# Where the stationary weight parts of the half-size matmuls begin in their buffers: four offsets become one

## Chip, cores and metric

The kernel runs on one core of a Trainium2 chip. The metric is the device time of one execution in microseconds (us), the median of several runs; lower is better. Three runs of the kernel before took 853.28, 854.75 and 855.66 us, so the median is 854.75 us.

## What is computed

One layer of a streaming encoder: a SwiGLU feed-forward block, a mixer (chunked attention beside a pooling branch), a second feed-forward block and a last norm, on 512 tokens of width 1024, with an inner width of 2816, all in float32.

```python
def swiglu_ffn(x, w_gate, w_up, w_down):
    return (jax.nn.silu(x @ w_gate) * (x @ w_up)) @ w_down

x = x + 0.5 * swiglu_ffn(rmsnorm(x, ffn1_norm[l]), ffn1_w_gate[l], ffn1_w_up[l], ffn1_w_down[l])
x = x + hybrid_mixer(rmsnorm(x, mix_norm[l]), w_in[l], q_norm[l], k_norm[l], rel_bias[l],
                     pool_w[l], pool_scale[l], w_out[l])
x = x + 0.5 * swiglu_ffn(rmsnorm(x, ffn2_norm[l]), ffn2_w_gate[l], ffn2_w_up[l], ffn2_w_down[l])
x = rmsnorm(x, final_norm[l])
```

The change touches the products `x @ w_gate` and `x @ w_up` of both feed-forward blocks.

## The kernel before

**High and low parts.** A float32 operand is split into a high part (rounded to the matmul's type, by ScalarE: `nc.scalar.copy`) and a low part (the remainder, by VectorE). A product of two operands is then three matmuls, `mm3` (lines 190 to 192): high by high, high by low, low by high. The first operand of each is stationary (loaded into TensorE by a weight load, "PEld" in the profile), the second moves through.

**The half-size up products.** The inner width has 22 panels of 128 columns. The first five (`PLAIN`) are multiplied as they stand: the weights are stationary, 128x128, and 512 tokens move. The other 17 of each block use a Strassen scheme (the Winograd form): seven products of half size in place of eight, where 128x128 weight parts are stationary and only 256 columns move. One pass of the loop over n (17 passes in each of the two feed-forward blocks) is called a block of matmuls here: seven products of 4 steps `k` of 3 matmuls, 84 matmuls. The weight operands of a block are four tiles, made by `high` (ScalarE, line 487) and `low` (VectorE, line 492):

- part 11: 512 columns, for the product A11
- part 13: 1024 columns (a sum of two quadrants), for S3 and S1
- part 24: 1024 columns (sums again), for S2 and A22
- part 22: 1024 columns, for A12 and S4

TensorE runs the products in the order A11 (part 11), S3 (13), S2 (24), A22 (24), S1 (13), A12 (22), S4 (22). Their moving operands are A11, A22, S1 and A12 in tiles that the profile calls `ha` (pool `norm`), S3 and S2 in `xa` (pool `resid`), and S4 in `sa` (the activations' pool). Outputs alternate between banks `mm` and `a`, so a profile row tells the products apart: `mm<-ha` is A11, S1 or A12, `a<-xa` S3, `mm<-xa` S2, `a<-ha` A22, `mm<-sa` S4.

**Buffers and order.** The four parts of a block take turns over four pairs of buffers of 1152 elements (`part_tiles`): three pairs in the pool `weights`, the fourth in the activations' pool (`act1` or `act2`), which begins behind the pool `small`. With four parts and four buffers, each part has the same buffer and the same offset in all 17 blocks of a layer. The order of all engines in this loop is written out by hand. While TensorE works on block n, ScalarE and VectorE prepare the parts of block n+1, and SyncE fetches the raw weights of block n+2 (two DMAs of 512 KB, lines 479 and 480, into two `raw` buffers in turn). GpSimd starts DMAs that add up weight panels in DRAM for the down products (line 720).

**The down products** come after the loop: there the tokens (`ah`) are stationary and the weight parts move, 512 columns at a time; these parts start at offset 0 of the same buffers.

Of the kernel before, what the change touches and what calls it, by code (L numbers as in the profile page):

```python
# [8 lines left out]
F32 = mybir.dt.float32  # L9
# [7 lines left out]
P = 128  # L17
# [18 lines left out]
HILO = 3  # L36


ROOM, STEPS = 1024 + 128, (16, 32, 64, 8)
PLAIN = 5  # L40
PROBS = 3
M_TILES = 16
# [25 lines left out]
def layer(  # L68
# [37 lines left out]
    tpool = ctx.enter_context(tc.tile_pool(name="temp", bufs=8))  # L106
    small = ctx.enter_context(tc.tile_pool(name="small", bufs=2))
    ps = ctx.enter_context(tc.tile_pool(name="ps", bufs=4, space=PSUM))
    dram = ctx.enter_context(tc.tile_pool(name="scratch", bufs=1, space=bass.MemoryType.DRAM))

    n_tiles = [0]
# [3 lines left out]
    def name(what):  # L115
        n_tiles[0] += 1
        return f"{what}_{n_tiles[0]}"

    def temp(dtype=F32):
        return tpool.tile([P, S], dtype, tag="t", name=name("t"))  # L120
# [43 lines left out]
    part_rooms: list = [(wpool, HILO)]  # L164
    n_parts = [0]

    def part_tiles(steps=(0,)):

        pool, bufs = part_rooms[n_parts[0] % len(part_rooms)]
        at = steps[n_parts[0] % len(steps)]  # L170
        n_parts[0] += 1
        return (
            pool.tile([P, ROOM], F32R, tag=tag, name=name("w" + tag), bufs=bufs)[:, at : at + 1024]
            for tag in ("hi", "lo")
        )

    def weights(src, parts=1):
        n = src.shape[-1]
        raw = raw_tile()
        hi, lo = part_tiles()  # L180
        for i in range(parts):
            part = slice(i * n // parts, (i + 1) * n // parts)
            nc.sync.dma_start(raw[:, part], src[:, part])
            split(raw[:, part], hi[:, part], lo[:, part])
        return hi, lo
# [240 lines left out]
    def ffn_up(norm, wA, down, loaded):  # L426
# [56 lines left out]
                )  # L483

        def high(n, what, src):
            hi, lo = (z[:, : src.shape[-1]] for z in part_tiles(STEPS))
            nc.scalar.copy(hi, src)  # L487
            w[what] = hi, lo, src

# [8 lines left out]
        def high11(n):  # L498
            if n < KF:
                high(n, (n, 11), raws[n][:, :S])  # L500
# [18 lines left out]
        def high13(n):  # L519
            if n < KF:  # L520
                high(n, (n, 13), w[n, "odd"])
# [5 lines left out]
        def high24(n):  # L527
            if n < KF:
                high(n, (n, 24), w[n, "even"])
# [61 lines left out]
        with tc.manual_schedule(engines={E.PE, E.DVE, E.Activation, E.SP}):  # L591
            last_silu = last_place = last_sums = nothing
            for n in range(PLAIN, KF):
                f = down.order[n]
                acc, up_lo, up_hi = bank()[:, :HT], bank()[:, :HT], abank()[:, :HT]
                u, z, sg = temp(), temp(), temp()
# [66 lines left out]
    class Down:  # L663
# [85 lines left out]
        def weights(self, i, g):  # L749

            if (i, g) in self.parts:
                return self.parts.pop((i, g))
            if (i, g) not in self.raws:
                self.fetch(i, g)
            src, raw = self.rows(i, g), self.raws.pop((i, g))
            n = groups[g][1] * S
            hi, lo = part_tiles()
            if tuple(src.shape[1:]) == (groups[g][1], S):
                split(raw, hi[:, :n], lo[:, :n])
            else:  # L760
                split(
                    raw.rearrange("p (d k c) -> p k d c", d=S // P, c=P),
                    *(z[:, :n].rearrange("p (k d c) -> p k d c", d=S // P, c=P) for z in (hi, lo)),
                )
            return hi, lo
# [722 lines left out]
    with tc.tile_pool(name="act2", bufs=1, reuse_waits="tile") as apool:  # L1488
        down2.begin(apool)

        for half in range(2):
            for t in range(NT):
# [5 lines left out]
                z = temp()  # L1498
# [229 lines left out]
```

## Time and profile before

| what | value |
|---|---|
| median of 3 runs | 854.75 us |
| the profiled execution's own time | 854.88 us |
| its span, first to last instruction | 852.9 us |
| granted TensorE clock | 0.998 of full speed |
| TensorE busy (matmuls) | 842.5 us, 99% |
| VectorE busy | 713.0 us, 84% |
| ScalarE busy | 502.0 us, 59% |
| GpSimd busy | 117.5 us, 14% |
| half-size blocks, first layer | from about 61.5 to 233 us of the span |
| half-size blocks, second layer | from about 569.5 to 739 us |

Read it from TensorE: its share of busy time is 99%, and in the chain of work that ended last 93% is TensorE. A matmul's busy time overlaps that of the next one, so what counts is not how long one is busy, but the distance from the start of one matmul to the start of the next. The timeline gives the starts in steps of 0.01 us.

### The profile page before, as it was taken

To read this page: it belongs to the slowest core of one execution; us is meant where nothing else is said; L and a number is where in the kernel's file an instruction comes from. 1 tells how busy PE (TensorE), PEld (TensorE's weight loads), DVE (VectorE), ACT (ScalarE), POOL (GpSimd) and SP (SyncE) were. 2 spreads that over 40 slices of the span, in tenths; PEclk is the share of its full clock that TensorE was granted. 3 is DMA by queue.
4 is the path that set the end of the run, shared out by engine and by line. 5 is a ranking of instruction groups with operands and counts; after the bars stand their busy time and mean duration, and the time that the engine had idled before them with its cause. 6 is when DMAs were issued, how large, how long until landed. Compare 5 with 4: busy or idle time off the path is not lost.

```text
span 852.9 us, 14106 instructions
## 1 busy us (share of the span) xinstructions
PE 842.5 (99%) x5288; PEld 757.1 (89%) x5288; DVE 713.0 (84%) x1122; ACT 502.0 (59%) x859; POOL 117.5 (14%) x196
## 2 busy tenths in 40 slices
PE   9999999999999999999999999999999999999996
PEld 8889999999988888887888888889999999978886
DVE  7998889888897868776979668988888888787896
ACT  7445555555576657458747746355555555666573
POOL 0124322222000000101111000122211111122000
PEclk9999999999999999999999999999999999999999
DMA  8199998877576864332212117249778767899832
GB/s 295 55 269 266 293 271 201 195 196 200 136 243 199 269 202 135 112 111 87 75 69 71 60 50 271 102 111 257 219 195 242 173 191 218 254 317 350 265 110 99
DMA packets 72244, 158.50 MB, mean 186 GB/s; under 512 B 6112, under 2 KB 29168, under 8 KB 71792
## 3 DMA queue, kind: packets, MB, share of 16 engines
q1 hardware_dynamic: 49088, 110.93, 37.5%
q0 software_dynamic: 22656, 46.14, 24.9%
q8 instruction: 41, 0.67, 0.3%
q10 hardware_dynamic: 432, 0.54, 0.2%
q14 instruction: 27, 0.22, 0.1%
HBM read 153.38 MB, written 50.34 MB: 239 GB/s over the span
## 4 chain that ended last, share of the span: by engine, by line
PE 93%; DMA 2%; DVE 2%; ACT 1%; issue 1%; SPq 0%; ACTq 0%; DVEq 0%
PE mm L190 22%; PE mm L191 22%; PE mm L192 22%; PE a L191 7%; PE a L192 7%; PE a L190 7%; DMA raw<-in_wA_dram 2%; PE a L1288 1%; PE a L1224 1%; PE a L1276 1%; DVE wlo L492 1%; PE a L227 0%; PE a L1495 0%; DVE wlo L146 0%; PE a L1146 0%
## 5 line engine op out<-in xcount | busy, mean ns | idle before, releaser
L145 ACT CAST whi<-raw 128x1024 fp32r<-128x1024 f32 (+2 forms) x115 | 107.4, 946 | 57.5 <-PE mm L191 17.0
L146 DVE TENSOR_TENSOR wlo<-raw,whi 128x1024 fp32r<-128x1024 f32 (+2 forms) x115 | 124.2, 1089 | 20.3 <-ACT whi L145 19.9
L191 PE MATMUL mm<-ha,whi 128*128 128x256 f32 x408 | 115.5, 283 | 0.0
L192 PE MATMUL mm<-ha,wlo 128*128 128x256 f32 x408 | 115.0, 282 | 0.0
L190 PE MATMUL mm<-ha,whi 128*128 128x256 f32 x408 | 114.9, 282 | 0.0
L583 ACT ACTIVATE t<-mm 128x256 f32<-128x256 f32 x102 | 39.2, 384 | 120.9 <-PE mm L192 120.1
L492 DVE TENSOR_TENSOR wlo<-wsum,whi 128x1024 fp32r<-128x1024 f32 x68 | 83.0, 1220 | 13.8 <-ACT whi L487 13.7
L192 PEld LDWEIGHTS mm<-ha,wlo 128*128 128x128 f32 x408 | 77.3, 189 | 0.0
L190 PEld LDWEIGHTS mm<-ha,whi 128*128 128x128 f32 x408 | 77.2, 189 | 0.1
L191 PEld LDWEIGHTS mm<-ha,whi 128*128 128x128 f32 x408 | 77.1, 189 | 0.1
L190 PE MATMUL mm<-hhi,whi 128*128 128x512 f32 x192 | 75.6, 396 | 0.0
L191 PE MATMUL mm<-hlo,whi 128*128 128x512 f32 x192 | 75.0, 391 | 0.0
L192 PE MATMUL mm<-hhi,wlo 128*128 128x512 f32 x192 | 74.7, 391 | 0.0
L720 POOL DMA_DIRECT2D wsum<-in_wB_dram x72 | 70.4, 1148 | 11.7 <-issue 8.2
L487 ACT CAST whi<-wsum 128x1024 fp32r<-128x1024 f32 x68 | 68.0, 1048 | 2.9 <-PE mm L191 2.7
L191 PE MATMUL mm<-wlo,ah 128*128 128x512 f32 x176 | 68.6, 390 | 0.0
L192 PE MATMUL mm<-whi,ah 128*128 128x512 f32 x176 | 68.5, 389 | 0.0
L190 PE MATMUL mm<-whi,ah 128*128 128x512 f32 x176 | 68.4, 390 | 0.0
L492 DVE TENSOR_TENSOR wlo<-raw,whi 128x512 fp32r<-128x512 f32 x68 | 62.6, 951 | 4.7 <-ACT whi L487 4.7
L718 POOL COPY mark<-t 128x1 f32<-128x1 f32 x40 | 14.1, 353 | 378.9 <-DVE t L628 229.6
L487 ACT CAST whi<-raw 128x512 fp32r<-128x512 f32 x68 | 56.3, 828 | 11.4 <-DMA raw<-in_wA_dram 11.4
L146 DVE TENSOR_TENSOR ah<-acts,ah 128x512 fp32r<-128x512 f32 (+1 forms) x72 | 45.7, 641 | 16.3 <-ACT ah L145 15.9
(228 smaller groups left out, 2378.5 us busy)
## 6 DMA issues: line engine op xcount, KB each, us to landing
raw<-in_wA_dram SPq DMA_DIRECT2D x87, 512.0 KB, 5.6
wsum<-in_wB_dram POOLq DMA_DIRECT2D x60, 512.0 KB, 7.5
raw<-wsum SPq DMA_DIRECT2D x40, 512.0 KB, 4.5
raw<-in_wB_dram SPq DMA_DIRECT2D x30, 512.0 KB, 4.7
wsum<-wsum POOLq DMA_DIRECT2D x20, 512.0 KB, 5.6
x<-in_xT_dram SPq DMA_DIRECT2D x16, 256.0 KB, 6.0
raw<-in_wQK_dram SPq DMA_DIRECT2D x8, 512.0 KB, 3.5
raw<-in_wO_dram SPq DMA_DIRECT2D x8, 512.0 KB, 3.4
```

Of the source, the lines that this page charges most:

```text
L145: nc.scalar.copy(hi, src)
L146: nc.vector.tensor_tensor(lo, src, hi.bitcast(F32), op=ALU.subtract)
L190: nc.tensor.matmul(acc, a[0], b[0], start=start, stop=False, **more)
L191: nc.tensor.matmul(acc, a[0], b[1], start=False, stop=False, **more)
L192: nc.tensor.matmul(acc, a[1], b[0], start=False, stop=stop, **more)
L487: nc.scalar.copy(hi, src)
L492: nc.vector.tensor_tensor(lo, src, hi.bitcast(F32), op=ALU.subtract)
L583: nc.scalar.activation(dst, src, AF.Copy, scale=scale)
L718: nc.gpsimd.tensor_copy(mark, after[:, 0:1])
L720: nc.gpsimd.dma_start(self.rows(i, g), self.rows(self.terms[i][at], g), **(dict(accum_op=ALU.add) if at else {}),)
L1224: nc.tensor.matmul(banks[i][:, at : at + n], qT[pair][0][a][rows, t * P : (t + 1) * P], kT[pair][0][b][rows, :n], start=a + b == 0, stop=a ...
L1276: nc.tensor.transpose(tp[:, n : n + P], prob[h, t][:, j * P : (j + 1) * P], ident)
```

## The change

The four offsets by turns become one: each part of the half-size products begins 16 elements (64 bytes) into its buffer. A tile of 64 float32 (256 bytes per partition) that nothing uses is set aside in the pool `small`, so that all that lies behind it, the activations' pool among it, moves up by 256 bytes.

```diff
-ROOM, STEPS = 1024 + 128, (16, 32, 64, 8)
+ROOM, AHEAD_OF_PARTS, ALIGN = 1024 + 128, 16, 64
...
     ps = ctx.enter_context(tc.tile_pool(name="ps", bufs=4, space=PSUM))
+    small.tile([P, ALIGN], F32, tag="align", name="align", bufs=1)
...
-    def part_tiles(steps=(0,)):
+    def part_tiles(at=0):
         pool, bufs = part_rooms[n_parts[0] % len(part_rooms)]
-        at = steps[n_parts[0] % len(steps)]
         n_parts[0] += 1
...
         def high(n, what, src):
-            hi, lo = (z[:, : src.shape[-1]] for z in part_tiles(STEPS))
+            hi, lo = (z[:, : src.shape[-1]] for z in part_tiles(AHEAD_OF_PARTS))
```

No instruction is added, removed or moved: on every engine the same instructions stand in the same order, and only addresses differ. In bytes per partition, as the two programs place them:

| operand | buffer | offset before, after | start modulo 512 before, after |
|---|---|---|---|
| part 11 (A11) | `weights` | 256, 64 | 128, 448 |
| part 13 (S3, S1) | activations' pool | 32, 64 | 160, 448 |
| part 24 (S2, A22) | `weights` | 64, 64 | 448, 448 |
| part 22 (A12, S4) | `weights` | 128, 64 | 0, 448 |
| moving `sa` (S4) | activations' pool | 0, 0 | 128, 384 |
| moving `ha`, `xa` | `norm`, `resid` | 0, 0 | 384, 384 |
| all else in the activations' pool and the mixer's, which takes its place | | | 128, 384 |

High and low tiles of a part start alike modulo 512. Part 24 is the one whose start stays where it was.

## Prediction

> **What bounds the kernel now.** I began with the page's table of busy time, then took busy time by stage, to see where TensorE ever waits. The first row below is the page's; the other three are stages, with their length, then the busy time of PE, PEld, DVE, ACT and POOL, the clock, the DMA share and GB/s.
>
> ```profile
> PE 842.5 (99%) x5288; PEld 757.1 (89%) x5288; DVE 713.0 (84%) x1122; ACT 502.0 (59%) x859; POOL 117.5 (14%) x196
> ...
> 70.50:82.30 11.80, 10.17 (x85) 9.97 (x85) 9.00 (x14) 5.40 (x11) 4.02 (x6) 1.00 1.10 309
> ...
> 112.50:232.00 119.50, 119.50 (x1009) 119.50 (x1008) 103.72 (x145) 66.82 (x121) 24.66 (x36) 1.00 0.80 197
> ...
> 568.00:738.00 170.00, 170.00 (x1428) 169.73 (x1427) 148.59 (x209) 95.96 (x172) 33.16 (x54) 1.00 0.75 201
> ```
>
> In the half-size blocks of the second layer (568 to 738) and in those of the first from 112.5 us on, PE is busy without a gap, at the full granted clock (1.00). VectorE has 87% there (103.72 of 119.50; 148.59 of 170.00), so nothing feeds TensorE late. Only near the loop's start does TensorE wait: 11.80 - 10.17 = 1.63 us at 70 to 82 us. So a change of the distance between matmuls in these blocks goes straight into the time.
>
> Next I read that distance from the timeline, for one block of the second layer. The columns are start, duration, engine, line, operation; each row is the first matmul of a product, in order A11, S2, S1, A12 and the next block's A11.
>
> ```profile
> 649.28 0.28 PE L190 MATMUL mm<-ha,whi 128*128 128x256 f32 x1
> ...
> 652.12 0.28 PE L190 MATMUL mm<-xa,whi 128*128 128x256 f32 x1
> ...
> 654.95 0.28 PE L190 MATMUL mm<-ha,whi 128*128 128x256 f32 x1
> ...
> 656.37 0.28 PE L190 MATMUL mm<-ha,whi 128*128 128x256 f32 x1
> ...
> 659.25 0.28 PE L190 MATMUL mm<-ha,whi 128*128 128x256 f32 x1
> ```
>
> A block takes 659.25 - 649.28 = 9.97 us. A11 and S3 together take 2.84 us, S2 and A22 2.83, S1 1.42, A12 and S4 2.88. All have 12 matmuls of one shape, so what differs is where operands lie. The pair that now begins 64 bytes into its buffers (S2, A22) is the shortest, 0.118 us a matmul; the pair 128 bytes in (A12, S4) the longest, 0.120. Within the long pair A12 takes its moving operand from `ha` and S4 from `sa`, which lie differently, and A22 and S1 both use `ha`, so I put the difference down to the stationary start.
>
> The Trainium skill, "TensorE: Matmul & The Clock Gate", section "Step-by-step: what each phase is for", says that the moving operand and the weight load have independent SBUF read ports, so that loading the next weights takes no bandwidth from the running matmul. By that rule a start offset would cost nothing and the time would stay; the 2.88 against 2.83 us above speaks against it.
>
> **The change part by part.** First, the steady distance. Five of seven products get the 64-byte start that S2 and A22 have. At 2.83 / 2 = 1.415 us a product a block becomes 7 x 1.415 = 9.905, at the rows' coarseness of 0.01 us 9.89 to 9.91 us, against 9.97: 0.06 to 0.08, I take 0.075 us. Over 34 blocks that is 2.55 us.
>
> Second, what is lost at the loop's start. These are rows of the chain of work that ended last (start, us, what), with the matmul that ended each of its two waits.
>
> ```profile
> 66.01 10.53 DMA raw<-in_wA_dram
> ...
> 77.57 0.38 PE a L190
> ...
> 96.86 9.94 DMA raw<-in_wA_dram
> ...
> 107.84 0.39 PE a L190
> ```
>
> Both waits hang on a raw-weight DMA of 10 us, not on matmuls. A faster TensorE reaches the same wait earlier and waits longer: of the first five blocks' 5 x 0.075 = 0.37 us I count 0.25 as lost, by what lies between each DMA's issue and its wait. With nothing else, 854.88 - 2.55 + 0.25 = 852.6 for the profiled execution.
>
> Third, and largest, a tighter distance that the 64-byte start allows. Here is A22, still the unchanged part 24, behind those waits: the first pair of rows lies behind the wait that ended at 77.57, eleven steps from the second matmul of A22 to the first of S1; the second pair, ten steps, is the same product two blocks later, after a delay of under 0.1 us; the third, four steps, lies behind the wait that ended at 107.84; the last pair is A12 and S4 of the block of the second pair.
>
> ```profile
> 77.80 0.28 PE L191 MATMUL a<-ha,whi 128*128 128x256 f32 x1
> ...
> 79.09 0.28 PE L190 MATMUL mm<-ha,whi 128*128 128x256 f32 x1
> ...
> 97.82 0.28 PE L191 MATMUL a<-ha,whi 128*128 128x256 f32 x1
> ...
> 98.95 0.28 PE L192 MATMUL a<-ha,wlo 128*128 128x256 f32 x1
> ...
> 108.77 0.28 PE L191 MATMUL a<-ha,whi 128*128 128x256 f32 x1
> ...
> 109.22 0.28 PE L192 MATMUL a<-ha,wlo 128*128 128x256 f32 x1
> ...
> 100.49 0.28 PE L190 MATMUL mm<-ha,whi 128*128 128x256 f32 x1
> ...
> 103.34 0.28 PE L190 MATMUL mm<-ha,whi 128*128 128x256 f32 x1
> ```
>
> The first runs at 1.29 / 11 = 0.117 us, the second at 1.13 / 10 = 0.113, the third at 0.45 / 4 = 0.113. So with the same addresses the stream has two distances, the steady 0.118 and a tight 0.113, and a hitch can move it from one to the other (here in two of three). The last pair shows that this state outlives the product: A12 and S4 take 2.85 us there in place of 2.88, and two blocks on the usual 2.88 is back. In the kernel before, tight running ends because the next product starts elsewhere. With all parts at 64 bytes nothing of that kind ends it. If it holds from 107.84 us to the end of the first layer's loop at about 233 us, that is 125 / 9.97 = 12.6 blocks, and a block of 84 x 0.113 = 9.49 us saves 0.48: 6.0 us. In the second layer no wait lies inside the loop, so I leave it at the steady 0.075 x 17 = 1.3 us. Sum: 6.0 + 1.3 + 0.1 (what is kept of the first blocks) = 7.4 us, 847.5 for the profiled execution, which lies 0.13 us above the median of the runs: **847.4**, taken as 847.5.
>
> The cover for it: at 9.49 us a block VectorE's 103.72 / 119.50 x 9.97 = 8.65 us would be 91%. If that cover fails, a tight block is as long as VectorE makes it; were it 9.7, the 6.0 would be 3.4. The transfers of a block fit too: the DMA share of 0.80 becomes 0.84.
>
> Fourth, the pool's move by 256 bytes. The down products read every fourth part from the activations' pool. These rows are the first matmuls of three successive parts: the second part lies in that pool (start 128 modulo 512), the first and the third in the pool `weights` (384).
>
> ```profile
> 265.94 0.39 PE L190 MATMUL a<-whi,ah 128*128 128x512 f32 x1
> ...
> 268.66 0.39 PE L190 MATMUL mm<-whi,ah 128*128 128x512 f32 x1
> ...
> 271.38 0.39 PE L190 MATMUL mm<-whi,ah 128*128 128x512 f32 x1
> ```
>
> The first two parts each take 2.72 us for 12 matmuls. What moves through TensorE may lie at either residue, and I put the move at 0. For the mixer's matmuls, some 450 whose tiles all move, no pair of rows differs in nothing but this; by the rows' step of 0.01 us in 12 matmuls, bounds of 0.4 us to either side. ScalarE's and VectorE's copies into the parts also change addresses; a nanosecond of each is covered by their idle 13% and more.
>
> **The rivals.** (a) *Tight in the second layer too.* A hitch is not the only way in: what precedes the second loop are 512-column matmuls, and no row shows a 64-byte product right behind them. Tight running there saves 17 x 0.48 = 8.2 in place of 1.3 us: 840.6; with VectorE as a brake, up to 845. Against it: behind the product S3, S2 starts at the steady distance in the rows above.
>
> (b) *Steady all through.* The first pair above stayed at 0.117 after a wait, so the state need not change: 854.75 - 2.3 = 852.4.
>
> (c) *The offset is not the cause.* The part and its offset are tied in every block, so the place in the order, or what ran ahead, could make A12 and S4 long; in the last pair above they took 2.85 at their old offset. Then at most S1, S3 and A11 gain 0.02 a block: 854.1 to 854.8. The rule of the Trainium skill told above, independent read ports, leads to the upper of these.
>
> (d) *Slower: all seven products fall into the long pattern.* Starts that agree everywhere could make each weight load meet the moving stream alike, as in A12 and S4 at 1.44 us. A block is then 7 x 1.44 = 10.08, 34 x 0.11 = 3.7 us more: 858.5. It decides once the five moved products average over (9.97 - 2.83) / 5 = 1.43 us. Against it: S2 and A22 keep 2.83 though they move different operands.
>
> **How the numbers follow.** Forecast 0.30, (a) 0.27, (b) 0.24, (c) 0.08, (d) 0.11. The likeliest gives 847.5. The range runs from (a) at 840.6 to (b) with the mixer's bound and the spread of the runs, 853.4; (c), (d) and the edges are left out, about 0.2. A measurement of this kernel can tell about 0.3%, 2.6 us, from no change. The forecast and (a) lie beyond it; (b) at 2.3 us lies next to it, with 0.11 beyond and 0.13 within. So faster is 0.30 + 0.27 + 0.11 = 0.68, same 0.13 + 0.08 = 0.21, slower 0.11.
>
> **What would show it.** In the timeline of the changed kernel a block of the second layer should take 9.90 us, each product 1.41 to 1.42, and A12 and S4 together 2.83: that is the first step. The blocks of the first layer after about 108 us should take 9.49: the third. The waits at 77 and 107 us should be longer by about 0.1 us. Down products should stay at 2.72 us. A second layer at 9.49 means (a); a first layer at 9.90 throughout means (b); 9.97 means (c). DVE waits in front of matmuls inside the loop would show that the cover failed. The forecast is wrong if the tight distance needs the old neighbours or ends within a block.

## The result, and the profile after

| what | before | after |
|---|---|---|
| median | 854.38 us (6 runs, 853.28 to 855.66) | 850.09 us (6 runs, 847.04 to 851.86) |
| ratio of the medians | | 0.9945, 95% interval 0.9922 to 0.9968 |
| the profiled execution, its span | 854.88 us, 852.9 us | 847.57 us, 845.6 us |
| TensorE busy | 842.5 us, 99% | 835.0 us, 99% |

The kernel is faster by 0.55%. The profiled execution hits the forecast's 847.5 us to 0.1 us, while the median of the runs lies 2.6 us above it; both have to be explained.

The first view is busy time in three stretches, before and then after: from the first layer's waits to near the end of its loop (72 to 223 us), the part of it behind the waits (126 to 223), and the second layer's loop (572 to 722). The columns are those of the prediction's table by stage; what is read here is PE's busy time and its count of matmuls, in brackets.

```profile
72.00:223.00 151.00, 149.29 (x1256) 148.86 (x1255) 131.82 (x184) 83.25 (x150) 37.17 (x53) 1.00 0.90 227
126.00:223.00 97.00, 97.00 (x819) 97.00 (x819) 85.53 (x120) 53.91 (x97) 19.69 (x28) 1.00 0.79 193
572.00:722.00 150.00, 150.00 (x1266) 150.00 (x1265) 133.14 (x185) 84.18 (x152) 29.55 (x48) 1.00 0.78 211
```

```profile
72.00:223.00 151.00, 149.29 (x1309) 148.85 (x1308) 137.37 (x192) 87.07 (x158) 37.34 (x53) 1.00 0.90 227
126.00:223.00 97.00, 97.00 (x859) 97.00 (x858) 89.63 (x126) 56.99 (x103) 19.80 (x28) 1.00 0.79 196
572.00:722.00 150.00, 150.00 (x1276) 150.00 (x1275) 133.96 (x188) 85.15 (x153) 28.07 (x48) 1.00 0.78 208
```

In the same time TensorE starts 40 matmuls more in the first layer (859 against 819) and 10 more in the second. A matmul is busy for 0.28 us, so a stretch counts some 2.4 that began before it; without them the distance from matmul to matmul is 97 / 816.6 = 0.1188 us before and 97 / 856.6 = 0.1132 after in the first layer, 150 / 1263.6 = 0.1187 and 150 / 1273.6 = 0.1178 in the second. The time that TensorE waits happens to be the same, 151.00 - 149.29 = 1.71 us in both; the experiments below show that it differs much from execution to execution. This way of reading one row, time over count, serves for every experiment below.

The timeline of after shows the same by product. First a block of the second layer, then one of the first behind the waits; the rows are the first matmuls of A11, S2, S1, A12 and the next A11, as in the prediction.

```profile
653.16 0.28 PE L190 MATMUL mm<-ha,whi 128*128 128x256 f32 x1
...
655.99 0.28 PE L190 MATMUL mm<-xa,whi 128*128 128x256 f32 x1
...
658.82 0.28 PE L190 MATMUL mm<-ha,whi 128*128 128x256 f32 x1
...
660.23 0.28 PE L190 MATMUL mm<-ha,whi 128*128 128x256 f32 x1
...
663.06 0.28 PE L190 MATMUL mm<-ha,whi 128*128 128x256 f32 x1
```

```profile
151.68 0.28 PE L190 MATMUL mm<-ha,whi 128*128 128x256 f32 x1
...
154.40 0.28 PE L190 MATMUL mm<-xa,whi 128*128 128x256 f32 x1
...
157.12 0.28 PE L190 MATMUL mm<-ha,whi 128*128 128x256 f32 x1
...
158.48 0.28 PE L190 MATMUL mm<-ha,whi 128*128 128x256 f32 x1
...
161.20 0.28 PE L190 MATMUL mm<-ha,whi 128*128 128x256 f32 x1
```

In the second layer all products are alike: 2.83, 2.83, 1.41 and 2.83 us, a block of 9.90. In the first they are alike and shorter: 2.72, 2.72, 1.36, 2.72, a block of 9.52. The same instructions, with starts that are alike modulo 512 bytes, thus run at two distances in one execution, 0.118 (called steady) and 0.113 us (tight).

What stands between the two is one long wait. The chain of waits of after has the raw-weight DMAs again, and the row below them is the first matmul behind the first of the two, with TensorE's wait in brackets. ScalarE, which is named there, had itself waited for that DMA, which landed at 76.15 + 10.67 = 86.82.

```profile
76.15 10.67 DMA raw<-in_wA_dram
...
97.08 9.93 DMA raw<-in_wA_dram
```

```profile
87.86 0.38 PE L190 MATMUL a<-ha,whi 128*128 128x256 f32 x1 [0.97 <-ACT t L583]
```

Up to that wait (the first two blocks) the blocks take 9.89 us. Behind it the stream is tight. The fourth and fifth block still contain a short delay and a second wait of 0.75 us; from the sixth block on each takes 9.52 to the loop's end. By block starts the first layer's loop shrinks from 171.7 to 165.1 us, the second's from 169.6 to 168.2. The rest of the span changes by under 0.7 us (336.2 to 336.3 between the loops, 113.9 to 113.3 behind them) save for the start, 61.5 to 62.7 us, which the change doesn't touch.

### The profile page after: what moved, and what is told of

It reads as the page before. It is cut to its first block, busy times and chain, and to the rows that moved or that the text cites. A ratio compares the mean times of both kernels' runs of the same rounds, so it can differ in the third digit from the quotient of the medians.

```text
span 845.6 us, 14106 instructions
## 1 busy us (share of the span) xinstructions
PE 835.0 (99%) x5288; PEld 748.7 (89%) x5288; DVE 712.7 (84%) x1122; ACT 501.8 (59%) x859; POOL 118.5 (14%) x196
## 4 chain that ended last, share of the span: by engine, by line
PE 93%; DMA 3%; DVE 1%; ACT 1%; issue 1%; SPq 0%; DVEq 0%; ACTq 0%
PE mm L190 22%; PE mm L192 22%; PE mm L191 22%; PE a L190 8%; PE a L191 7%; PE a L192 7%; DMA raw<-in_wA_dram 2%; PE a L1288 1%; PE a L1224 1%; PE a L1276 1%; DMA x<-in_xT_dram 1%; DVE wlo L492 1%; PE a L1495 0%; PE a L1146 0%; PE a L307 0%
## 5 line engine op out<-in xcount | busy, mean ns | idle before, releaser
L190 PE MATMUL mm<-ha,whi 128*128 128x256 f32 x408 | 113.8, 279 | 0.0
L191 PE MATMUL mm<-ha,whi 128*128 128x256 f32 x408 | 113.8, 279 | 0.0
```

The lines of the kernel that those rows point to most:

```text
L190: nc.tensor.matmul(acc, a[0], b[0], start=start, stop=False, **more)
L191: nc.tensor.matmul(acc, a[0], b[1], start=False, stop=False, **more)
```

## The experiments

Two questions were open: is it the offset (and not the pool's move, or the product's place in the order), and what makes the stream tight or steady. Every kernel below keeps the whole computation; where a matmul is added, nothing uses its product. "Narrow" stands for one added matmul of 64 moving columns. The rows are those of the view by stretches, read as above.

### 1. The offsets without the pool's move

After, without the tile that moves the pool:

```diff
-    small.tile([P, ALIGN], F32, tag="align", name="align", bufs=1)
```

> The changed kernel without the 256-byte tile: all parts begin 64 bytes in, the activations' pool stays where it was. Theory (the stationary start modulo 256 sets the distance, the pool's place nothing): a block of the second layer takes 9.89 us as in the changed kernel, the first layer goes to 9.52 behind its waits, 850 us. Rival (the moved pool matters, since part 13 and the moving tile sa lie in it): S3, S1 and S4 stay at their old length, a second-layer block takes 9.92 to 9.95 us, no block of 9.52, 853 us.

Measured: median 848.92 us (7 runs, 846.83 to 852.61), ratio 0.9942 (0.9921 to 0.9963). The profiled execution took 852.37 us.

```profile
126.00:223.00 97.00, 97.00 (x823) 96.81 (x823) 86.10 (x122) 54.48 (x99) 19.68 (x28) 1.00 0.80 192
572.00:722.00 150.00, 150.00 (x1276) 150.00 (x1275) 134.26 (x188) 83.89 (x151) 29.05 (x48) 1.00 0.80 213
```

The second layer is as in after, x1276, though part 13 now begins at 192 modulo 512 and not at 448 like the others. In the first layer this execution is steady, 823 in place of 859: it turned tight behind a wait of 0.77 us in its third block, stayed so behind a short delay in the fourth, and turned steady again behind a wait of 0.91 us in its fifth. So the offset alone brings the gain, and the state in the first layer is not the same in each execution. Steady from there to the end it took 170.2 us for the loop, 5.1 more than after's profiled execution, and 852.37 against 847.57 us in all.

### 2. The pool's move without the offsets

Before, with the same tile of 256 bytes:

```diff
+    small.tile([P, 64], F32, tag="align", name="align", bufs=1)
```

> The kernel before with the 256-byte tile alone, the four old offsets kept. Theory: blocks of 9.97 us in both layers, 854.4 us, within 0.1% of before. Rival (the pool's place matters): blocks shorter than 9.95 us, under 853 us.

Measured: median 854.94 us (12 runs), ratio 1.0006 (0.9995 to 1.0016).

```profile
572.00:722.00 150.00, 150.00 (x1266) 150.00 (x1265) 133.11 (x186) 83.72 (x151) 29.25 (x48) 1.00 0.79 211
```

The row has before's 1266. The move does nothing that can be measured.

### 3. A restart of an empty TensorE in the second layer

After, with one matmul in the second layer's first block that must wait for a tile which ScalarE has just written:

```diff
-                acc, up_lo, up_hi = bank()[:, :HT], bank()[:, :HT], abank()[:, :HT]
+                acc, up_lo, spare = bank()[:, :HT], bank()[:, :HT], abank()
+                up_hi = spare[:, :HT]
...
                 copy(u[:, :HT], acc)
+                if loaded and n == PLAIN:
+                    nc.tensor.matmul(
+                        spare[:, HT : HT + 1], u[:, :P], ones[:, 0:1], start=True, stop=True
+                    )
                 product(up_hi, cut(w13, S, S), S3, True)
```

> The changed kernel with one more matmul of one column in the first half-size block of the second layer, which reads a tile that ScalarE has just copied (its product is not used), so that TensorE runs empty for about 0.8 us and starts anew. Theory (a restart from empty puts the 64-byte stream into the tight distance, which then lasts): the second layer's blocks take 9.52 in place of 9.89 us, 17 x 0.37 = 6.3 us less and about 1 us more for the wait, 845 us. Rival (the tight distance belongs to the first layer, its DMA traffic or its buffers): blocks stay at 9.89, 851 us.

Measured: median 849.71 us (844.44 to 851.24), ratio 0.9937 (0.9915 to 0.9960). The timeline at the added matmul (L607), and the second and twelfth matmul of S3 behind it:

```profile
568.22 0.38 PE L607 MATMUL a<-ones,t 128*128 128x1 f32 x2 [1.13 <-ACT t L583]
...
568.66 0.28 PE L191 MATMUL a<-xa,whi 128*128 128x256 f32 x1
...
569.84 0.28 PE L192 MATMUL a<-xa,wlo 128*128 128x256 f32 x1
```

```profile
572.00:722.00 150.00, 150.00 (x1276) 150.00 (x1275) 132.77 (x186) 83.57 (x150) 26.96 (x45) 1.00 0.79 213
```

TensorE ran empty for 1.13 us and then took 1.18 us for ten steps, 0.118 each; the loop has the steady 1276. So a restart from empty does not make the stream tight each time, as the theory had it. Whether it does so sometimes stays open: this is one execution, and another of the six took 844.44 us, 2.6 us less than the fastest of after, and left no trace.

### 4. One narrow matmul in the second layer, with no wait

Made as the control of the last one: at the same place a matmul that reads what has long been there.

```diff
                 copy(u[:, :HT], acc)
+                if loaded and n == PLAIN:
+                    nc.tensor.matmul(
+                        spare[:, HT : HT + 64], w13[0][:, S : S + P],
+                        norm.a[S3][0][0][:, :64], start=True, stop=True,
+                    )
                 product(up_hi, cut(w13, S, S), S3, True)
```

> The changed kernel with one narrow matmul (64 moving columns, product not used) at the same place of the second layer, which waits for nothing. Theory (the weight load must have fallen behind an empty TensorE): no change, blocks of 9.89 us, 850 us. Rival (any irregular step moves the state): blocks of 9.52 us, 844 us.

Measured: median 847.21 us (2 runs, 846.39 and 848.03), ratio 0.9917 (0.9897 to 0.9938). The narrow matmul, the first one behind it, and two matmuls twelve steps apart:

```profile
569.46 0.20 PE L607 MATMUL a<-xa,whi 128*128 128x64 f32 x1
569.50 0.36 PE L190 MATMUL a<-xa,whi 128*128 128x256 f32 x1
...
570.16 0.28 PE L192 MATMUL a<-xa,wlo 128*128 128x256 f32 x1
...
571.52 0.28 PE L192 MATMUL mm<-xa,wlo 128*128 128x256 f32 x1
```

```profile
72.00:223.00 151.00, 145.34 (x1266) 144.42 (x1265) 132.61 (x186) 83.56 (x152) 37.33 (x53) 1.00 0.89 225
...
572.00:722.00 150.00, 150.00 (x1326) 150.00 (x1325) 139.09 (x197) 87.84 (x157) 31.21 (x51) 1.00 0.81 215
```

The control is what turned the stream: 1.36 us for twelve steps at once, 0.113 each, and 1326 matmuls where steady ones make 1276. The theory, that nothing would change, fell. The loop took 162.0 us in place of 168.2. This is rival (a)'s second layer, brought about by 64 columns. The first layer, which this edit does not touch, shows what a tight stream can run into: 151.00 - 145.34 = 5.66 us of waits in place of 1.71. Its longest is this one, 197.70, and it hangs on a raw-weight DMA of 11.57 us:

```profile
197.70 0.39 PE L190 MATMUL a<-ha,whi 128*128 128x256 f32 x1 [2.51 <-ACT t L583]
```

```profile
185.09 11.57 DMA raw<-in_wA_dram
```

### 5 to 8. Other offsets, and the old ones, with the narrow matmul

The next four ran once each; the kernel before took 855.78 us on that chip. All have the narrow matmul of the last one. Three change the one offset (in elements of 4 bytes); the fourth is before, with its four offsets, plus the narrow matmul.

```diff
-ROOM, AHEAD_OF_PARTS, ALIGN = 1024 + 128, 16, 64
+ROOM, AHEAD_OF_PARTS, ALIGN = 1024 + 128, 0, 64
```

> All four parts at offset 0 (start 384 modulo 512, 128 modulo 256), the pool moved, and the narrow matmul of the run before in the second layer. Theory (the stationary start sets the steady distance whatever the product): all seven products alike, near the old A11 (start 128 modulo 256) at 1.42 to 1.43 us, a block 9.95 to 10.0 us; the narrow matmul leaves no lasting tight distance. Rival (the product's place sets it): A12 and S4 stay the longest at 1.44 and S2 and A22 the shortest at 1.41, a block 9.97.

Measured with the offset 0: 858.74 us.

```profile
572.00:722.00 150.00, 150.00 (x1252) 150.00 (x1252) 131.44 (x183) 83.35 (x151) 29.57 (x48) 1.00 0.78 208
```

150 / 1249.6 = 0.1200 us, a block of 10.08, all seven products at 1.44, and the narrow matmul changes nothing that lasts. All products are alike, as the theory had it, but longer than the 1.42 to 1.43 that it took from the old A11. This is the distance of rival (d), at another start than the change's.

```diff
+ROOM, AHEAD_OF_PARTS, ALIGN = 1024 + 128, 8, 64
```

> All four parts 32 bytes in (start 160 modulo 256), the pool moved, and the narrow matmul in the second layer. Theory: all seven products like the old S3 and S1, 1.42 us, a block 9.94 us, and no lasting tight distance at this start. Rival (place): unequal products as in the kernel before, a block 9.97.

Measured with 32 bytes: 854.9 us.

```profile
572.00:722.00 150.00, 150.00 (x1270) 150.00 (x1270) 133.47 (x186) 84.42 (x154) 29.55 (x48) 1.00 0.79 211
```

150 / 1267.6 = 0.1183 us, 1.420 a product: what S3 and S1 had before at the same start. No tight stretch.

```diff
+ROOM, AHEAD_OF_PARTS, ALIGN = 1024 + 128, 64, 64
```

> All four parts 256 bytes in (64 elements; start 128 modulo 256 as at offset 0), the pool moved, and the narrow matmul in the second layer. Theory (only the start modulo 256 counts): the same blocks as with offset 0, 9.95 to 10.0 us. Rival (the start within a larger stretch counts): blocks that differ from those at offset 0 by over 0.02 us.

Measured with 256 bytes, which is the same start as offset 0 modulo 256: 857.1 us.

```profile
572.00:722.00 150.00, 150.00 (x1253) 150.00 (x1252) 131.44 (x184) 83.25 (x150) 29.64 (x48) 1.00 0.77 209
```

The count of offset 0, within one. Moving by 256 bytes changes nothing in the distance; moving by 64 does.

> The kernel before, four offsets, with the narrow matmul in the second layer. Theory (the tight distance needs one start for all parts, since the other starts do not keep it): blocks back at 9.97 us within one block, 854.5 us. Rival (a narrow matmul alone makes the stream tight): blocks under 9.7 us, 849 us.

Measured with the four old offsets and the narrow matmul: 854.36 us.

```profile
572.00:722.00 150.00, 150.00 (x1265) 150.00 (x1265) 133.00 (x185) 83.98 (x151) 29.38 (x48) 1.00 0.79 211
```

Before's count, within one. With starts that change from product to product the narrow matmul has no lasting effect, and neither had it with all parts at 128 or 160 modulo 256. Of the kernels so far only those with all parts at 64 bytes stay tight.

### 9. Narrow matmuls in both layers

The fourth kernel's matmul, in the first half-size block of both layers:

```diff
-                if loaded and n == PLAIN:
+                if n == PLAIN:
```

> The changed kernel with the narrow matmul in the first half-size block of both layers. Theory (a narrow step can move the 64-byte stream into the tight distance, and it lasts until the next wait): the second layer at 9.52 us a block, the first at 9.52 up to its first DMA wait and decided anew at each wait; 844 us, and a spread of some us from the first layer. Rival (the one run with a narrow matmul was tight by chance): the second layer at 9.89 in the profile, 850 us.

Measured: median 843.31 us (4 runs, 841.66 to 844.50), ratio 0.9867 (0.9848 to 0.9887).

```profile
72.00:223.00 151.00, 148.61 (x1304) 147.82 (x1303) 136.34 (x190) 86.02 (x156) 37.46 (x53) 1.00 0.89 227
126.00:223.00 97.00, 97.00 (x858) 97.00 (x857) 89.28 (x125) 56.76 (x103) 19.83 (x28) 1.00 0.78 192
572.00:722.00 150.00, 149.78 (x1321) 149.58 (x1321) 137.84 (x193) 87.93 (x159) 29.59 (x48) 1.00 0.80 212
```

Both layers run tight, with 2.39 us of waits in the first stretch. That the state would be decided anew at each wait didn't show: behind each of the four waits of the first layer (0.30 to 0.74 us) and the one of the second (0.22 us) the stream was tight again.

### 10 and 11. Fewer weight sums beside the first layer's loop

The waits at the loop's start hang on raw-weight DMAs that run beside GpSimd's sums in DRAM. Here these sums go at the usual rate for the whole loop, without the higher rates at its start. First after with this edit alone, then with the ninth kernel's matmuls too.

```diff
-    ..., block1, [4] * (PLAIN - 2) + [3] * 6 + [2] * 9
+    ..., block1
```

> The changed kernel with 2 weight sums per block on the GpSimd queue in the first layer in place of 4, 3 and 2 (36 in the loop in place of 48, the rest later), so that the raw-weight DMAs near the loop's start have less beside them. Theory (the waits are DMA waits, and only a wait lets the stream become tight): the waits shrink or go, the first layer stays at 9.89 us a block throughout if they go; 850 us with a narrower spread than the changed kernel. Rival (the stream becomes tight by itself in the first layer): blocks of 9.52 without a wait ahead of them, 846 us.

Measured without the matmuls: median 851.74 us (12 runs, 846.25 to 855.03), ratio 0.9968 (0.9951 to 0.9986).

```profile
72.00:223.00 151.00, 151.00 (x1284) 151.00 (x1283) 135.09 (x188) 85.73 (x154) 31.17 (x46) 1.00 0.81 204
...
572.00:722.00 150.00, 150.00 (x1276) 150.00 (x1276) 134.25 (x188) 84.14 (x151) 28.29 (x47) 1.00 0.79 215
```

In this execution TensorE never waits in the loop, and never turns tight: 151 / 1281.6 = 0.1178 in the first layer too. So the waits were removed, and the gain of the first layer went with them. The narrower spread that was expected did not come: its 12 runs span 8.8 us, the six of after 4.8. What the others did, the fastest of 846.25 us among them, no trace shows. The stretch between the loops grows by 1.3 us, where the sums are made that were put off.

> Both edits: 2 sums per block, and the narrow matmul in the first half-size block of both layers. Theory: 9.52 us a block in both layers and waits of under 1 us, 34 x 0.45 = 15.4 us below the kernel before, 838 to 840 us. Rival (a tight first layer waits for its DMAs whatever the sums): waits of some us in the first layer, 843 us or more.

Measured with them: median 842.92 us (4 runs, 839.72 to 844.64), ratio 0.9859 (0.9838 to 0.9880).

```profile
72.00:223.00 151.00, 151.00 (x1335) 151.00 (x1334) 137.09 (x193) 88.43 (x159) 33.68 (x49) 1.00 0.84 212
...
572.00:722.00 150.00, 150.00 (x1326) 150.00 (x1326) 136.16 (x193) 86.98 (x158) 29.94 (x49) 1.00 0.80 213
```

No wait and both layers tight, 51 and 50 matmuls more than the kernel above in the same stretches; each loop takes 162.0 us. This execution, the fastest of the four, took 839.72 us, within the 838 to 840 expected. The other three took 842.83 to 844.64 us, nearer to the rival's 843, and left no trace. This and the ninth kernel are the fastest, 1.3 to 1.4% below before and, by the two ratios, some 0.8 to 0.9% below the change. Their intervals overlap, so that fewer sums help once both are tight is not shown.

### 12. 96 bytes

```diff
-ROOM, AHEAD_OF_PARTS, ALIGN = 1024 + 128, 16, 64
+ROOM, AHEAD_OF_PARTS, ALIGN = 1024 + 128, 24, 64
```

> All four parts 96 bytes in (24 elements, start 224 modulo 256), the pool moved, and the narrow matmul in the second layer: a start that no kernel so far has. Theory (the distance follows from the start modulo 256 alone): seven equal products. By the two starts beside it, 64 bytes (1.413, or tight 1.360) and 128 bytes (about 1.44 in the kernel before), 1.36 to 1.44 us each; it says which of the two sides it belongs to, and whether tight running lasts there. Rival (the product's place counts): unequal products.

Measured, once, with the fourth kernel's matmul in the second layer: 853.03 us, the kernel before 854.51 (median) on that chip.

```profile
572.00:722.00 150.00, 150.00 (x1280) 150.00 (x1280) 134.65 (x189) 84.71 (x154) 29.67 (x48) 1.00 0.79 212
```

150 / 1277.6 = 0.1174 us: the shortest steady distance of all the starts tried, but the narrow matmul does not make it tight. 64 bytes stays the best.

This start has two distances too, and here the second is the longer one. In the first layer, behind a wait of 0.98 us that ended at 107.66 us, the products take 1.42 to 1.43 us until the next wait, two blocks on. These are the first matmuls of two successive blocks there:

```profile
113.46 0.28 PE L190 MATMUL mm<-ha,whi 128*128 128x256 f32 x1
...
123.44 0.28 PE L190 MATMUL mm<-ha,whi 128*128 128x256 f32 x1
```

This block takes 9.98 us, against 84 x 0.1174 = 9.86 elsewhere. So a wait does not always make a stream faster.

## Why the prediction was right, and what was off

**The number: in part luck.** In the profiled execution the two loops saved 6.6 + 1.4 = 8.0 us, 0.6 more than the 7.4 forecast. The kernel's start, which the change doesn't touch, took 1.2 us more and the part behind the loops 0.6 us less; with these the sum is 7.3. That the hit is within 0.1 us is chance, and so is that this execution was tight from 87.86 us to the end of the first loop. Of the gain forecast for the median, 854.75 - 847.5 = 7.25 us, 4.3 us came.

**The steady distance: right.** 2.83 us a pair and 9.90 a block stood in the forecast, and after shows both. The cause is the start of the stationary part, not the place in the order, so rival (c) fell: with one start all products are alike, and the distance follows the start. Each row below but that of 64 bytes rests on single executions, all with the narrow matmul.

| offset of all parts | start modulo 256 | matmuls in 150 us | distance, us |
|---|---|---|---|
| 0, 256 | 128 | 1252, 1253 | 0.1200 |
| 32 | 160 | 1270 | 0.1183 |
| 64 | 192 | 1276; tight 1326 | 0.1178; tight 0.1133 |
| 96 | 224 | 1280 | 0.1174 |

What is shown of the 256 is that moving by 256 bytes changes nothing. A pattern that repeats after 128 bytes would fit as well: A12 and S4 took 1.44 us before at 0 modulo 256, like the parts at 128. One value does not fit into the table: A11 took 1.427 us before at 128 modulo 256, where all parts together at that start take 1.44. What ran ahead of it began elsewhere, so neighbours may matter a little too; no run tests that alone.

**The lost part of the first blocks: not decided, and rather too small.** 0.25 us was counted, and each of the two waits was to grow by about 0.1. Before and after both have 1.71 us of waits from 72 to 223 us, but at other places: 1.63 us at 77.57 before, 0.97 at 87.86 and 0.75 at 108.04 after. Such a pair says little. The three traced executions with the four old offsets (before, the second and the eighth experiment) have 0.82 to 1.71 us of waits in this stretch; the four with all parts at 64 bytes and nothing added there (after and the first, third and fourth) have 1.68 to 5.66. As far as these seven tell, the faster stream waits more, as was argued, and by more than 0.25 us; part of that belongs to the tight stream.

**The tight first layer: right in the profiled execution, mis-sized for the median.** The forecast took it as holding from 107.84 us to the loop's end, 12.6 blocks of 0.48 us. The profile has it from the wait at 87.86 us; twelve blocks of 9.52 save 9.97 - 9.52 = 0.45 each, the shorter stretches before them bring the loop to 6.6 us less, against 6.0 + 0.1 forecast. But the prediction gave the state a single course, and it has several: in the four profiled executions with waits in the first layer and no matmul added there (after and the first, third and fourth experiments) the stream ran tight behind 12 of 16 waits and steady behind 4. Of the 11 waits of 0.48 us and more it was tight behind 10; of the 5 short delays of 0.1 to 0.3 us, behind 2. The first experiment ended steady, at 852.37 us, close to rival (b)'s 852.4; after's profiled execution is one of its two fastest of six. So what rival (b) describes occurs as well as what the forecast does. The step that was mis-sized for the median is the term of 6.0 us, which took the tight state as holding to the loop's end in every execution. The median of 850.1 lies between the two ends. That the other runs of after mix tight and steady stretches is argued from this, since they left no trace.

**The second layer steady: right, and for the reason given.** No wait lies in the loop, and it saved 169.6 - 168.2 = 1.4 us against 1.3 forecast. That only a disturbance changes the state is borne out from both sides, as far as traces go: without waits the first layer stayed steady too (one execution of the tenth experiment), and in all five loops with a narrow matmul at 64 bytes (one of the fourth, two each of the ninth and eleventh) the stream was tight from there on. Rival (a) was thus a true state of the second layer that the change does not enter.

**The slower rival (d): a true distance at a wrong start.** All products at 1.44 is what 0 and 256 bytes give, 858.74 and 857.1 us; the argument against it, that S2 and A22 keep 2.83 with different operands, decided rightly.

**The cover: held, but another one is thin.** VectorE is busy for 89.63 of 97.00 us in the tight stretch, 92% where 91% was worked out. What held a tight loop up was the raw-weight DMA, as in the 5.66 us of waits of the fourth experiment; the prediction had looked at the DMA share only.

**The pool's move and the down products: right, at nothing.** The second experiment has 1.0006, the part between the loops, with the mixer in it, changes by 0.1 us, and the first matmuls of three parts of after are 2.72 us apart, as before:

```profile
260.65 0.39 PE L190 MATMUL a<-whi,ah 128*128 128x512 f32 x1
...
263.37 0.39 PE L190 MATMUL mm<-whi,ah 128*128 128x512 f32 x1
...
266.09 0.39 PE L190 MATMUL mm<-whi,ah 128*128 128x512 f32 x1
```

**What stays open.** Why a narrow matmul turned the stream tight each time, an empty TensorE did not in the one execution with a trace, and a DMA wait does so mostly but not always. One idea would be that the weight load of the next matmul meets the moving stream at another moment in the two states. The weight loads' rows (PEld) do not show it. Here is a matmul of after and the weight load that starts beside it, first steady and then tight:

```profile
653.28 0.28 PE L191 MATMUL mm<-ha,whi 128*128 128x256 f32 x1
653.29 0.19 PEld L192 LDWEIGHTS mm<-ha,wlo 128*128 128x128 f32 x1
...
151.79 0.28 PE L191 MATMUL mm<-ha,whi 128*128 128x256 f32 x1
151.80 0.19 PEld L192 LDWEIGHTS mm<-ha,wlo 128*128 128x128 f32 x1
```

In both states the load starts within 0.01 us of the matmul and takes 0.19 us, so at this resolution they look alike. The tight state was seen to last at the 64-byte start alone: at 128, 160 and 224 modulo 256 neither the narrow matmul nor the waits of the first layer (five of 0.18 to 1.44 us at the first two starts, three of 0.72 to 0.98 us at the third) brought a distance near 0.113.

## What to carry to other kernels

Where TensorE is the bound and few columns move per weight load, time over count in a stretch without waits is the first number to take: if products of one shape differ, try other starts of the stationary operand within 256 bytes, and give all of them the same one. Which start is best was measured here for one shape only, 128x128 parts with 256 moving columns. Take that number along the whole loop and in more than one execution, since a distance can have two states that outlast what set them. And when TensorE gets faster, look at the DMAs that end its waits before the engines that are busiest.

## What the hardware showed that was not expected

The same 128x128 by 256 matmuls have distances from 0.1133 to 0.1200 us, 6% apart, by nothing but the stationary start and the stream's history. The Trainium skill, "TensorE: Matmul & The Clock Gate", section "Step-by-step: what each phase is for", has the weight load on an SBUF read port of its own, so that it takes no read bandwidth from the running matmul. The prediction drew from it that a start costs nothing. That is not so here: the steady rows of the table above run from 0.1174 to 0.1200 us. Whether the two reads disturb each other or the weight load alone depends on its start, no run here separates.

A single matmul of 64 columns, 0.04 us of TensorE's time by its rows (569.46 to 569.50), saved 6.2 us in the loop behind it (168.2 to 162.0), and an execution without waits can be the slower one: the tenth experiment's profiled execution, without a wait in either loop, took 851.68 us, the change's, with 1.71 us of waits, 847.57. That taking the waits away costs time on the whole isn't shown: the medians are 851.74 and 850.09 us, and the intervals of their ratios overlap.
